# Plain down products for the first token group, down operands made by the second, and four weight sums in three instructions

## The chip, the cores and the metric

The kernel runs on one core of a Trainium2 chip. The metric is the device time of one launch in microseconds, as the median of several runs. The core has TensorE (PE, with its weight loads listed as PEld), VectorE (DVE), ScalarE (ACT) and GpSimd (POOL). SyncE (SP) issues most DMA transfers.

## The reference

The reference is one layer of a hybrid decoder: a mixer with three kinds of heads, then a dense SwiGLU feed-forward part. It works on 2048 prompt tokens with 16 meta tokens ahead of them, and on a sample group of 8 x 4 tokens, with a model width of 1024 and a feed-forward width of 2816. The change is in the feed-forward part alone:

```python
def _swiglu(hn, w_ffn_in, w_ffn_out):
    g, u = jnp.split(hn @ w_ffn_in, 2, axis=-1)
    return (jax.nn.silu(g) * u) @ w_ffn_out
# in _trunk, after the mixer:
h = h + _swiglu(_rmsnorm(h, norm_ffn[l]), w_ffn_in[l], w_ffn_out[l])
```

Inputs and outputs are float32.

## The kernel before

**Precision.** Each operand of a large product is kept as two float16 parts, a high part and the remainder, made by `split_w` (L154): ACT writes the high part (L155) and DVE the remainder (L156). A product is three passes, `PASSES`: high with high, high with low, low with high.

**Fewer products.** The feed-forward products use a 2 x 2 block scheme (Strassen in Winograd's form) with seven block products in place of eight. Seven operands belong to each side: three plain blocks (A11, A12, A22 or B11, B21, B22) and four sums (S1 to S4 or T1 to T4). `left` (L1013) forms the four sums of a gate/up weight tile and `right` (L1021) those of a down weight tile or of the activations, each with four POOL instructions of 128 x 256 elements. `operands` then splits the plain blocks, the last block and the sums.

**Groups.** The 17 token tiles are worked in three groups: tiles 1 to 6, tiles 7 to 12, and tile 0 (48 rows) with tiles 13 to 16. Tiles stand in pairs, so that half a group is 384, 384 and 280 columns. For each group the feed-forward width is cut into four parts of 2, 3, 3 and 3 blocks (`PARTS`), each block being 256 wide. A part has two phases:

- For each block, `hidden` calls `quad` twice, for gate and up. A `quad` runs seven products of 12 matmuls each (L1239) into PSUM banks, with activations as the moving operand, and combines them on ACT, DVE and POOL (L1244 to L1252; L1248 and L1249 are POOL's). `hidden` then applies silu (L1259), multiplies (L1262), forms S1 to S4 of the result on POOL (L1274 to L1280) and splits all seven operands into `hh` (L1268 on ACT, L1269 on DVE).
- For each half m of the output width and each pair of tiles, `down` (L1285) runs seven products (L1292) with `hh` as the stationary and the down weights as the moving operand, 256 columns each. It combines the results into the residual tile `xr` with ACT copies (L1302, L1305), DVE (L1303, L1304, L1324 to L1328) and POOL (L1326, L1329, L1330).

This text calls the place where a part goes from the first phase to the second a turn.

**Weights.** `gu_operands` gives two `w` tiles of 7 KB per partition for each quad, `dn_operands` one tile for each block and half. Both go through `kept`: in the first group the tile is made from the raw weights, used, and written to a DRAM scratch (`wgu_scratch`, `wdn_scratch`). In the later groups it is read back. The raw tiles, the sums and the `w` tiles come from one pool at the left of SBUF. It has 6 raw, 2 sums and 6 `w` buffers in the first group. A new pool with 11 `w` buffers alone is opened ahead of the second group and serves the third too. All these loads and stores are issued by SP, in order.

**Order.** The instructions of each engine stand in a fixed order that a planner writes with its own cost model, from the program order and from the time at which it thinks that operands and buffers are ready. At run time each engine takes its queue in that order.

The activations' operands `x2` are read for the next group while the last part of a group runs (`load_x2`). The residual tiles `xr` are read from a scratch and stored by POOL's queue at the end of a group. In the first two parts of the first group `prep_late` prepares the activations of the last two pairs.

Of the kernel before, what the change touches and what calls it, by code (L numbers as in the profile page):

```python
# [8 lines left out]

F32 = mybir.dt.float32  # L10
F16 = mybir.dt.float16
BF16 = mybir.dt.bfloat16
I32 = mybir.dt.int32
AF = mybir.ActivationFunctionType
# [45 lines left out]
def trunk(ctx, tc, I, O, groups):  # L60
# [4 lines left out]
    def nm(s):  # L65
        n_names[0] += 1
        return f"{s}_{n_names[0]}"
# [933 lines left out]

    A11, A12, A22, S1, S2, S3, S4 = range(7)
    B11, B21, B22, T1, T2, T3, T4 = range(7)

# [3 lines left out]
            split_w(src, hi, lo, scale)  # L1010
        return w

    def left(w, s, a11, a12, a21, a22, plain, scale):  # L1013
        s1, s2, s3, s4 = (s[:, i].rearrange("p (k c) -> p k c", c=a11.shape[-1]) for i in range(4))
        G.tensor_tensor(s1, a21, a22, op=ALU.add)
        G.tensor_tensor(s2, s1, a11, op=ALU.subtract)
        G.tensor_tensor(s3, a11, a21, op=ALU.subtract)
        G.tensor_tensor(s4, a12, s2, op=ALU.subtract)
        return operands(w, plain, a22, s, scale)

    def right(w, s, b11, b12, b21, b22, plain, scale):  # L1021
        G.tensor_tensor(s[:, 0], b12, b11, op=ALU.subtract)
        G.tensor_tensor(s[:, 1], b22, s[:, 0], op=ALU.subtract)
        G.tensor_tensor(s[:, 2], b22, b12, op=ALU.subtract)
        G.tensor_tensor(s[:, 3], b21, s[:, 1], op=ALU.subtract)
        return operands(w, plain, b22.unsqueeze(1), s, scale)

    def pairs(grp):
        big = [t for t in grp if t]
# [80 lines left out]

    pg_cm = tc.tile_pool(name="pg", bufs=1, side="left", reuse_waits="tile")
    pg = [pg_cm.__enter__()]
    w_bufs = [6]

    def raw_tile():
        return pg[0].tile([P, 4, 256], F32, tag="raw", bufs=6, name=nm("raw"))

    def w_full():
        return pg[0].tile([P, 2, 7, 256], F16, tag="w", bufs=w_bufs[0], name=nm("w"))

    def w_tile():
        w = w_full()
# [2 lines left out]
    def sum_tile():  # L1125
        return pg[0].tile([P, 4, 256], F32, tag="sums", bufs=2, name=nm("sums"))

    def kept(dram, make):

        w = w_full()  # L1130
        parts = [w[:, 0], w[:, 1]]
        if w_bufs[0] == 6:
            make(parts)
            nc.sync.dma_start(dram, w.rearrange("p a o c -> p (a o c)"))
        else:
            nc.sync.dma_start(w.rearrange("p a o c -> p (a o c)"), dram)
        return parts
# [4 lines left out]
    def prep_few(x, pst):  # L1142

        L = T0
        n = L // 2
        z2 = [w_full().rearrange("p a o c -> p (a o c)")[:, : 28 * n] for _ in range(2)]

        def put(op, v):
            v = v.rearrange("p (q k) n -> p q k n", q=2)
            hi, lo = (z.rearrange("p (q o k n) -> p q o k n", q=2, o=7, k=2)[:, :, op] for z in z2)  # L1150
            S.activation(hi, v, AF.Copy)
            V.tensor_tensor(lo, v, hi, op=ALU.subtract)

        b12, t1, t2, t3 = (tmp()[:, : 4 * n].rearrange("p (j n) -> p j n", n=n) for _ in range(4))
        for q in range(2):
            ps = pst().rearrange("p (j n) -> p j n", n=P)
            for j in range(4):
                T.transpose(ps[:, j, :L], x[:L, (4 * q + j) * P : (4 * q + j + 1) * P], ident[:L, :L])
            pv = ps[:, :, :n], ps[:, :, n:L]
            if q == 0:  # L1160
                S.activation(b12, pv[1], AF.Copy)
                put(B11, pv[0])
                V.tensor_tensor(t1, b12, pv[0], op=ALU.subtract)
                put(T1, t1)
            else:
                put(B21, pv[0])
                put(B22, pv[1])
                V.tensor_tensor(t2, pv[1], t1, op=ALU.subtract)
                put(T2, t2)
                V.tensor_tensor(t3, pv[1], b12, op=ALU.subtract)  # L1170
# [8 lines left out]
    def gu_operands(c0):  # L1179

        rows = w_gu[:, c0 : c0 + 256].rearrange("(h q k p) c -> q h p k c", h=2, q=2, p=P)

        def make(w, q):
            raw = raw_tile()
            for h in range(2):
                nc.sync.dma_start(raw[:, 2 * h : 2 * h + 2], rows[q, h])
            a = [[raw[:, 2 * h : 2 * h + 2, u * P : (u + 1) * P] for h in range(2)] for u in range(2)]
            left(w, sum_tile(), a[0][0], a[0][1], a[1][0], a[1][1], raw[:, :, 0:P], WG)

        return [kept(wgu_d[c0 % DFF // 256, c0 // DFF, q], lambda w: make(w, q)) for q in range(2)]  # L1190

    def dn_operands(jq, m):


        def make(w):
# [3 lines left out]
            right(w, sum_tile(), raw[:, 0], raw[:, 1], raw[:, 2], raw[:, 3], raw.rearrange("p (k h) c -> p h k c", k=2)[:, 0], WS)  # L1199

        return kept(wdn_d[jq, m], make)

    gu_first = [gu_operands(c) for c in (0, DFF)]
    interleave(outs)
# [4 lines left out]
    with (  # L1209
# [20 lines left out]
        def quad(A, n):  # L1230
# [15 lines left out]
            V.tensor_tensor(r21, prod(S3, T3), r12, op=ALU.add)  # L1246
            S.activation(r22, prod(S1, T1), AF.Copy)  # L1247
            G.tensor_tensor(r12, r12, r22, op=ALU.add)  # L1248
            G.tensor_tensor(r22, r22, r21, op=ALU.add)  # L1249
            V.tensor_tensor(r11, prod(A12, B21), r11, op=ALU.add)  # L1250
# [4 lines left out]
        def hidden(q, jq, n):  # L1255
# [15 lines left out]
            put(A11, a11)  # L1271
            put(A12, a12)
            put(A22, a22)
            G.tensor_tensor(s1, a21, a22, op=ALU.add)  # L1274
            put(S1, s1)
            G.tensor_tensor(s2, s1, a11, op=ALU.subtract)
# [4 lines left out]
            put(S4, s4)  # L1281

        PRODS = ((A11, B11), (S2, T2), (S3, T3), (S1, T1), (A12, B21), (A22, T4), (S4, B22))

        def down(ws, x1, x2_, c, off, L):  # L1285

# [57 lines left out]
        put_off = [pr for pr in all_pairs[early:] if pr[0]] + [[0]]  # L1344

        for gi, grp in enumerate(groups):
            if gi == 1:
                pg_cm.__exit__(None, None, None)
                pg_cm = tc.tile_pool(name="ph", bufs=1, side="left", reuse_waits="tile")
                pg[0] = pg_cm.__enter__()  # L1350
                w_bufs[0] = 11
            n = half[gi]

            rows2 = [[(pr[0], 0, P), (pr[1], 0, P)] if len(pr) == 2 else [(0, 0, T0 // 2), (0, T0 // 2, T0 // 2)] for pr in pairs(grp)]
# [6 lines left out]
            for q0, q1 in PARTS:  # L1361
# [345 lines left out]
```

## Time and profile before

| what | value |
|---|---|
| median of 3 runs | 2410.7 us (2409.39 to 2413.79) |
| the profiled execution | 2401.93 us, span of its instructions 2399.9 us |
| PE busy | 2215.4 us, 92% |
| DVE busy | 1673.4 us, 70% |
| POOL busy | 1148.9 us, 48% |
| ACT busy | 941.8 us, 39% |
| granted TensorE clock, mean | 0.973 |
| moved by DMA | 364.95 MB, 152 GB/s |

In the profile a line number is a line of the kernel, `out<-in` are the program's names without buffer numbers, and an arrow behind an idle time names what ended it. Busy matmuls overlap, so the mean length of one is more than the distance from one to the next. The feed-forward part starts at 1034.6 us of the span. The groups change at 1589.4 and 2043.4 us.

### The profile page before, as it was taken

How to read it: one execution, taken by the hardware profiler on the slowest of the kernel's cores; microseconds unless marked ns; L12 is line 12 of the kernel's file. 1: busy time of each engine (PE TensorE's matmuls, PEld its weight loads, DVE VectorE, ACT ScalarE, POOL GpSimd, SP SyncE). 2: the span in 40 equal slices, each digit the busy share in tenths (PEclk: the TensorE clock that was granted, in tenths of full speed). 3: DMA queues.
4: the chain of work that ended last, by engine and by line, in shares of the span. 5: the costliest groups of instructions: out<-in, count | busy, mean ns of one | idle time of the engine just before them, and what ended most of it. 6: DMA issues, size and time to landing. Idle time of an engine off the chain costs nothing. (4 is left out here: it accounts for less than half of the span.)

```text
span 2399.9 us, 51972 instructions
## 1 busy us (share of the span) xinstructions
PE 2215.4 (92%) x20298; PEld 1605.7 (67%) x20298; DVE 1673.4 (70%) x4064; ACT 941.8 (39%) x2526; POOL 1148.9 (48%) x1595
## 2 busy tenths in 40 slices
PE   6999999999999899787989979789999999999996
PEld 6677767767777445444657566567686867888886
DVE  8789888988988776558778687655454535655546
ACT  7455545545445432334343434422212122332323
POOL 7333233333333364559768787634332324544435
PEclk9999999999999999898999989999999999999998
DMA  7233333333323755995536545684334247744441
GB/s 259 46 67 70 67 74 62 75 65 80 66 65 83 188 192 181 304 305 193 188 140 216 190 169 203 178 305 174 123 121 157 108 168 194 272 176 172 181 166 39
DMA packets 294328, 364.95 MB, mean 152 GB/s; under 512 B 203807, under 2 KB 234479, under 8 KB 294066
## 3 DMA queue, kind: packets, MB, share of 16 engines
q1 hardware_dynamic: 285090, 331.02, 44.2%
q0 software_dynamic: 4384, 15.93, 1.7%
q10 hardware_dynamic: 4608, 14.68, 1.6%
q8 instruction: 159, 2.61, 0.4%
q14 instruction: 87, 0.71, 0.1%
HBM read 212.24 MB, written 103.50 MB: 132 GB/s over the span
## 5 line engine op out<-in xcount | busy, mean ns | idle before, releaser
L1239 PE MATMUL s<-x,w 128*128 128x384 f16 (+1 forms) x5544 | 827.8, 312 | 20.4 <-DMA w<-wgu_scratch 7.8
L1239 PEld LDWEIGHTS <-w 128*128 128x128 f16 x5544 | 543.2, 98 | 302.8 <-issue 19.0
L1292 PE MATMUL dn<-w,hh 128*128 128x256 f16 (+1 forms) x4158 | 446.6, 279 | 54.8 <-ACT hh L1268 21.8
L1292 PEld LDWEIGHTS <-hh 128*128 128x128 f16 (+1 forms) x4158 | 380.6, 99 | 119.6 <-issue 29.5
L212 PEld LDWEIGHTS <-xT 128*128 128x128 f16 (+1 forms) x1992 | 176.1, 99 | 188.6 <-issue 18.2
L1268 ACT ACTIVATE hh<-tmp 128x384 f16<-128x384 f32 (+1 forms) x231 | 112.4, 494 | 282.7 <-DVE tmp L1262 167.4
L1248 POOL TENSOR_TENSOR tmp<-tmp,tmp 128x384 f32<-128x384 f32 (+1 forms) x66 | 67.1, 1017 | 276.3 <-ACT tmp L1247 272.8
L1269 DVE TENSOR_TENSOR hh<-tmp,hh 128x384 f16<-128x384 f32 (+1 forms) x231 | 143.4, 628 | 75.7 <-ACT hh L1268 74.0
L212 PE MATMUL wo<-wo,xT 128*128 128x512 f16 x768 | 176.3, 387 | 7.6 <-DVE xn L992 3.0
L156 DVE SCALAR_TENSOR_TENSOR w<-raw,w 128x512 f16<-128x512 f32 (+1 forms) x136 | 108.5, 830 | 14.2 <-ACT w L155 14.2
L553 POOL TENSOR_TENSOR t<-t 128x8 f32<-128x8 f32 (+2 forms) x100 | 24.9, 249 | 188.2 <-DVE k L551 100.6
L1250 DVE TENSOR_TENSOR tmp<-s,tmp 128x384 f32<-128x384 f32 (+1 forms) x66 | 34.2, 519 | 108.4 <-PE s L1239 108.4
L212 PE MATMUL d<-xT,qf 128*128 128x128 f16 (+1 forms) x1632 | 107.4, 220 | 0.0
L156 DVE SCALAR_TENSOR_TENSOR w<-sums,w 128x1024 f16<-128x1024 f32 x68 | 98.5, 1450 | 9.5 <-ACT w L155 9.4
L1259 ACT ACTIVATE tmp<-tmp 128x384 f32<-128x384 f32 (+1 forms) x132 | 61.6, 490 | 109.0 <-DVE tmp L1250 51.7
L1324 DVE SCALAR_TENSOR_TENSOR xr<-dn,xr 128x256 f32<-128x256 f32 x192 | 78.9, 417 | 35.0 <-PE dn L1292 30.8
L212 PE MATMUL d<-xT,bqk 128*128 128x128 f16 (+1 forms) x1632 | 100.1, 220 | 3.3 <-DVE e L278 3.3
L212 PEld LDWEIGHTS <-qf 128*128 128x128 f16 x1632 | 95.2, 100 | 7.2 <-issue 2.1
L212 PEld LDWEIGHTS <-bqk 128*128 128x128 f16 x1632 | 93.0, 99 | 5.5 <-issue 4.6
L212 PE MATMUL d<-aig,xT 128*128 128x512 f16 (+1 forms) x408 | 92.7, 379 | 3.4 <-DVE g L358 3.4
L212 PE MATMUL d<-bvo,xT 128*128 128x512 f16 (+1 forms) x408 | 95.6, 380 | 0.2 <-DVE qlo L325 0.2
L212 PE MATMUL d<-xT,cq 128*128 128x128 f16 (+1 forms) x1632 | 94.8, 217 | 0.0
(536 smaller groups left out, 4044.2 us busy)
## 6 DMA issues: line engine op xcount, KB each, us to landing
w<-wgu_scratch SPq DMA_DIRECT2D x88, 896.0 KB
wgu_scratch<-w SPq DMA_DIRECT2D x44, 896.0 KB
w<-wdn_scratch SPq DMA_DIRECT2D x44, 896.0 KB
raw<-in_w_ffn_in_dram SPq DMA_DIRECT2D x88, 256.0 KB
wdn_scratch<-w SPq DMA_DIRECT2D x22, 896.0 KB
xs<-in_x_prompt_dram SPq DMA_DIRECT2D x26, 512.0 KB
x_scratch<-pT ACTq DMA_DIRECT2D x28, 448.0 KB
raw<-in_w_ffn_out_dram SPq DMA_DIRECT2D x22, 512.0 KB
```

The source lines that it names most:

```text
L156: V.scalar_tensor_tensor(lo, src, scale, hi, op0=ALU.mult, op1=ALU.subtract)
L212: T.matmul(out, lh(k, a), rh(k, b), start=(n == 0), stop=(n == 3 * nk - 1))
L553: G.tensor_tensor(tn, tv[:, :, :, 0], tv[:, :, :, 1], op=ALU.mult)
L1239: T.matmul(out, A[k // 2][p][:, a, k % 2 * P : k % 2 * P + P], x2[r][:, k // 2, op, k % 2, :n], start=i == 0, stop=i == 11)
L1248: G.tensor_tensor(r12, r12, r22, op=ALU.add)
L1250: V.tensor_tensor(r11, prod(A12, B21), r11, op=ALU.add)
L1259: S.activation(d, d, AF.Silu, scale=UF)
L1268: S.activation(hi, v, AF.Copy)
L1269: V.tensor_tensor(lo, v, hi, op=ALU.subtract)
L1292: T.matmul(out, hh[p][:, q, a, off : off + L], ws[q][r][:, b], start=(q, p, r) == order[0], stop=(q, p, r) == order[-1])
L1324: V.scalar_tensor_tensor(x[:L, cc], m, UD, x[:L, cc], op0=ALU.mult, op1=ALU.add)
```

## The change

- In the first group the down product is plain. `down_plain` computes both tiles of a pair with 512 output columns at a time: for each of the two tiles, each block, each half k of a block and each pass one matmul of 512 columns. One DVE instruction per tile and half adds the result to `xr`. For this the weights are only split (4 of 7 places of a `w` tile), and `hidden` returns after splitting A11, A12, A22 and A21 (in the place of S1).
- The second group makes the seven down operands from the raw weights, as the first did before, and writes them to the scratch. The third group reads them.
- The pools follow: the first stage is as it was, the second has 8 `w`, 3 raw and 2 sums buffers, and a third pool with 11 `w` buffers is opened ahead of the third group.
- The sums of a gate/up weight tile are made by three POOL instructions: one of 128 x 512 elements writes two of them, with a hand-written access pattern, and two of 128 x 256 follow. Two of the sums have the other sign, so `right`, `prep_few` and the pairs in `quad` change signs and places. The sums of a down weight tile are made by three in the same way (`right_of`).

```diff
-    def left(w, s, a11, a12, a21, a22, plain, scale):
-        s1, s2, s3, s4 = (...)
-        G.tensor_tensor(s1, a21, a22, op=ALU.add)
-        G.tensor_tensor(s2, s1, a11, op=ALU.subtract)
-        G.tensor_tensor(s3, a11, a21, op=ALU.subtract)
+    def left(w, s, raw, scale):
+        s3, s2, s4 = (s[:, i].rearrange("p (k c) -> p k c", c=P) for i in (0, 1, 3))
+        a11, a12, a21, a22 = (raw[:, 2 * h : 2 * h + 2, u * P : (u + 1) * P] for u in range(2) for h in range(2))
+        both = AP(a11.tensor, a11.offset, [a11.ap[0], (2 * 256 + P, 2), (256, 2), (1, P)])
+        G.tensor_tensor(s[:, 0::2].rearrange("p i (k c) -> p i k c", c=P), bc(a21, 1, 2), both, op=ALU.subtract)
+        G.tensor_tensor(s2, a22, s3, op=ALU.subtract)
         G.tensor_tensor(s4, a12, s2, op=ALU.subtract)
...
+    def right_of(w, s, b, plain, scale):
+        G.tensor_tensor(s[:, 0::2], b[:, 1::2], b[:, 0:2], op=ALU.subtract)
+        G.tensor_tensor(s[:, 1], b[:, 0], s[:, 2], op=ALU.add)
+        G.tensor_tensor(s[:, 3], b[:, 2], s[:, 1], op=ALU.subtract)
+        return operands(w, plain, b[:, 3].unsqueeze(1), s, scale)
...
-    w_bufs = [6]
+    stage, raw_bufs, w_bufs = [0], [6, 3], [6, 8, 11]
...
     def dn_operands(jq, m):
...
+        if stage[0] == 0:
+            w = w_tile()
+            split_w(load().rearrange("p a c -> p (a c)"), *(z[:, 0:4].rearrange("p a c -> p (a c)") for z in w), WS)
+            return w
+        return kept(wdn_d[jq, m], make, 1)
...
-            V.tensor_tensor(r21, prod(S3, T3), r12, op=ALU.add)
-            S.activation(r22, prod(S1, T1), AF.Copy)
+            V.tensor_tensor(r21, prod(S1, T3), r12, op=ALU.add)
+            S.activation(r22, prod(S3, T1), AF.Copy)
...
             put(A22, a22)
+            if stage[0] == 0:
+                put(A21, a21)
+                return
...
+        def down_plain(ws, x1, x2_, c, off):
+            order = [(q, k, p, r) for q in range(len(ws)) for k in range(2) for p, r in PASSES]
+            for x, ops in ((x1, (A11, A12)), (x2_, (A21, A22))):
+                out = pbt("dn")
+                for o in order:
+                    q, k, p, r = o
+                    T.matmul(out, hh[p][:, q, ops[k], off : off + P], ws[q][r][:, 2 * k : 2 * k + 2].rearrange("p h c -> p (h c)"), start=o == order[0], stop=o == order[-1])
+                V.scalar_tensor_tensor(x[:, c : c + 512], out, UD, x[:, c : c + 512], op0=ALU.mult, op1=ALU.add)
...
-            if gi == 1:
+            if gi:
                 pg_cm.__exit__(None, None, None)
-                pg_cm = tc.tile_pool(name="ph", bufs=1, side="left", reuse_waits="tile")
+                pg_cm = tc.tile_pool(name=f"ph{gi}", bufs=1, side="left", reuse_waits="tile")
                 pg[0] = pg_cm.__enter__()
-                w_bufs[0] = 11
+                stage[0] = gi
...
-                        down(ws, xr[ra], xr[rb], c.start, offs[ra[0]][1], ra[2])
+                        if gi == 0:
+                            down_plain(ws, xr[ra], xr[rb], c.start, offs[ra[0]][1])
+                        else:
+                            down(ws, xr[ra], xr[rb], c.start, offs[ra[0]][1], ra[2])
```

More of the change, by code (lines that the diff above doesn't have):

```diff
@@ L8 @@
 from concourse._compat import with_exitstack
+from concourse.ap import AP
 F32 = mybir.dt.float32
@@ L1011, in operands @@
         return w
-    def left(w, s, a11, a12, a21, a22, plain, scale):
-        s1, s2, s3, s4 = (s[:, i].rearrange("p (k c) -> p k c", c=a11.shape[-1]) for i in range(4))
-        G.tensor_tensor(s1, a21, a22, op=ALU.add)
-        G.tensor_tensor(s2, s1, a11, op=ALU.subtract)
-        G.tensor_tensor(s3, a11, a21, op=ALU.subtract)
+    def left(w, s, raw, scale):
[4 more added lines that the diff above has]
+        G.tensor_tensor(s2, a22, s3, op=ALU.subtract)
         G.tensor_tensor(s4, a12, s2, op=ALU.subtract)
-        return operands(w, plain, a22, s, scale)
+        return operands(w, raw[:, :, 0:P], a22, s, scale)
     def right(w, s, b11, b12, b21, b22, plain, scale):
         G.tensor_tensor(s[:, 0], b12, b11, op=ALU.subtract)
-        G.tensor_tensor(s[:, 1], b22, s[:, 0], op=ALU.subtract)
-        G.tensor_tensor(s[:, 2], b22, b12, op=ALU.subtract)
+        G.tensor_tensor(s[:, 1], b22, s[:, 0], op=ALU.add)
+        G.tensor_tensor(s[:, 2], b22, b12, op=ALU.add)
         G.tensor_tensor(s[:, 3], b21, s[:, 1], op=ALU.subtract)
         return operands(w, plain, b22.unsqueeze(1), s, scale)
+    def right_of(w, s, b, plain, scale):
[3 more added lines that the diff above has]
+        return operands(w, plain, b[:, 3].unsqueeze(1), s, scale)
     def pairs(grp):
@@ L1112, in trunk @@
     pg = [pg_cm.__enter__()]
-    w_bufs = [6]
+    stage, raw_bufs, w_bufs = [0], [6, 3], [6, 8, 11]
     def raw_tile():
-        return pg[0].tile([P, 4, 256], F32, tag="raw", bufs=6, name=nm("raw"))
+        return pg[0].tile([P, 4, 256], F32, tag="raw", bufs=raw_bufs[stage[0]], name=nm("raw"))
     def w_full():
-        return pg[0].tile([P, 2, 7, 256], F16, tag="w", bufs=w_bufs[0], name=nm("w"))
+        return pg[0].tile([P, 2, 7, 256], F16, tag="w", bufs=w_bufs[stage[0]], name=nm("w"))
     def w_tile():
@@ L1126, in sum_tile, with kept @@
         return pg[0].tile([P, 4, 256], F32, tag="sums", bufs=2, name=nm("sums"))
-    def kept(dram, make):
+    def kept(dram, make, when):
         w = w_full()
         parts = [w[:, 0], w[:, 1]]
-        if w_bufs[0] == 6:
+        if stage[0] == when:
             make(parts)
@@ L1167, in prep_few @@
                 put(B22, pv[1])
-                V.tensor_tensor(t2, pv[1], t1, op=ALU.subtract)
+                V.tensor_tensor(t2, pv[1], t1, op=ALU.add)
                 put(T2, t2)
-                V.tensor_tensor(t3, pv[1], b12, op=ALU.subtract)
+                V.tensor_tensor(t3, pv[1], b12, op=ALU.add)
                 put(T3, t3)
@@ L1186, in make, with load @@
                 nc.sync.dma_start(raw[:, 2 * h : 2 * h + 2], rows[q, h])
-            a = [[raw[:, 2 * h : 2 * h + 2, u * P : (u + 1) * P] for h in range(2)] for u in range(2)]
-            left(w, sum_tile(), a[0][0], a[0][1], a[1][0], a[1][1], raw[:, :, 0:P], WG)
-        return [kept(wgu_d[c0 % DFF // 256, c0 // DFF, q], lambda w: make(w, q)) for q in range(2)]
+            left(w, sum_tile(), raw, WG)
+        return [kept(wgu_d[c0 % DFF // 256, c0 // DFF, q], lambda w: make(w, q), 0) for q in range(2)]
     def dn_operands(jq, m):
-        def make(w):
+        def load():
             raw = raw_tile()
@@ L1198, in make @@
             nc.sync.dma_start(raw.rearrange("p (k h) c -> p k (h c)", k=2), w_dn[2 * jq * P : 2 * jq * P + 2 * P, c].rearrange("(k p) c -> p k c", p=P))
-            right(w, sum_tile(), raw[:, 0], raw[:, 1], raw[:, 2], raw[:, 3], raw.rearrange("p (k h) c -> p h k c", k=2)[:, 0], WS)
-        return kept(wdn_d[jq, m], make)
+            return raw
+        def make(w):
+            raw = load()
+            right_of(w, sum_tile(), raw, raw.rearrange("p (k h) c -> p h k c", k=2)[:, 0], WS)
+        if stage[0] == 0:
[3 more added lines that the diff above has]
+        return kept(wdn_d[jq, m], make, 1)
     gu_first = [gu_operands(c) for c in (0, DFF)]
@@ L1283, in trunk @@
         PRODS = ((A11, B11), (S2, T2), (S3, T3), (S1, T1), (A12, B21), (A22, T4), (S4, B22))
+        A21 = S1
+        def down_plain(ws, x1, x2_, c, off):
[6 more added lines that the diff above has]
+                V.scalar_tensor_tensor(x[:, c : c + 512], out, UD, x[:, c : c + 512], op0=ALU.mult, op1=ALU.add)
         def down(ws, x1, x2_, c, off, L):
```

## Prediction, made before the changed kernel was run

> **What bounds the kernel now.** I read the busy times by stage first, to find where TensorE (PE) is not the limit, then the groups of instructions inside those stages, then the order of single instructions at one place where PE stops. The first view is busy time by stretch: PE, PEld, DVE, ACT, POOL, then granted clock, DMA share, GB/s. The rows are the feed-forward part of the first, second and third group of tokens.
>
> ```profile
> 1034.60:1589.40 554.80, 480.57 (x3243) 324.29 (x3241) 415.97 (x640) 223.88 (x444) 429.43 (x447) 0.93 0.58 197
> 1589.40:2043.40 454.00, 453.65 (x3235) 316.83 (x3236) 219.21 (x427) 107.45 (x233) 152.53 (x175) 1.00 0.47 167
> 2043.40:2399.90 356.50, 337.71 (x3236) 283.18 (x3233) 199.13 (x431) 110.38 (x281) 155.37 (x207) 0.98 0.45 169
> ```
>
> The first two groups give PE the same products, yet the first takes 100.8 us longer. The second is PE alone: 453.65 of 454.00 us busy at clock 1.00. The groups of instructions, first group ahead of second, say which products pay (busy, mean ns, then idle before and its releasers):
>
> ```profile
> L1239 PE MATMUL s<-x,w 128*128 128x384 f16 x1848 | 304.3, 327 | 12.6 <-DMA x<-x_scratch 7.3 <-DVE tmp L1252 2.8 <-DVE tmp L1246 2.1
> L1292 PE MATMUL dn<-w,hh 128*128 128x256 f16 x1386 | 176.6, 291 | 53.9 <-ACT hh L1268 21.8 <-DVE hh L1269 8.8 <-DVE xr L1324 6.9
> ...
> L1239 PE MATMUL s<-x,w 128*128 128x384 f16 x1848 | 302.6, 327 | 7.8 <-DMA w<-wgu_scratch 7.8
> L1292 PE MATMUL dn<-w,hh 128*128 128x256 f16 x1386 | 152.3, 273 | 0.3 <-DVE hh L1269 0.3
> ```
>
> The gate/up products (L1239) differ by 1.7 us busy and 5.3 us of idle beyond a start wait of 7.3 us. The down products (L1292) differ by 24.3 us busy (slow clock, waits inside groups) and 53.6 us idle. Another 7.8 us is the wait that ends the first group and that the view books to the second. So the time is lost where a part turns from gate/up to down. One such turn, from the instructions in order of time:
>
> ```profile
> 1383.45 0.82 PE L1292 MATMUL dn<-w,hh 128*128 128x256 f16 x6
> 1390.54 1.04 PE L1292 MATMUL dn<-w,hh 128*128 128x256 f16 x4 [5.75 <-ACT hh L1268]
> 1395.13 7.68 PE L1292 MATMUL dn<-w,hh 128*128 128x256 f16 x55 [3.55 <-DVE hh L1269]
> 1404.85 5.12 PE L1292 MATMUL dn<-w,hh 128*128 128x256 f16 x30 [2.04 <-ACT hh L1268]
> ...
> 1386.44 1.70 POOL L1023 TENSOR_TENSOR sums<-raw,sums 128x256 f32<-128x256 f32 x1
> 1391.27 0.72 POOL L1025 TENSOR_TENSOR sums<-raw,sums 128x256 f32<-128x256 f32 x1
> 1391.95 0.99 POOL L1248 TENSOR_TENSOR tmp<-tmp,tmp 128x384 f32<-128x384 f32 x1
> ...
> 1385.83 1.74 DVE L156 SCALAR_TENSOR_TENSOR w<-sums,w 128x1024 f16<-128x1024 f32 x1
> 1394.04 0.56 DVE L1262 SCALAR_TENSOR_TENSOR tmp<-tmp,tmp 128x384 f32<-128x384 f32 x1 [4.12 <-POOL tmp L1249]
> ```
>
> PE waits for hh. hh waits for the last gate/up combination (POOL L1248, then DVE L1262), and that stands in POOL's queue behind the sums of down weights (L1022 to L1025), in DVE's behind their splits (L156). The second group has the same hh chain and no operand making, and PE passes the same turn without a stop:
>
> ```profile
> 1755.77 41.43 PE L1292 MATMUL dn<-w,hh 128*128 128x256 f16 x378
> ```
>
> **The change, part by part.** Prices for the first group (means under that load):
>
> ```profile
> L156 DVE SCALAR_TENSOR_TENSOR w<-sums,w 128x1024 f16<-128x1024 f32 x64 | 92.6, 1448 | 6.1 <-ACT w L155 6.0
> L156 DVE SCALAR_TENSOR_TENSOR w<-raw,w 128x512 f16<-128x512 f32 x64 | 58.1, 907 | 13.7 <-ACT w L155 13.6
> L156 DVE SCALAR_TENSOR_TENSOR w<-raw,w 128x256 f16<-128x256 f32 x64 | 47.2, 737 | 0.0
> L1023 POOL TENSOR_TENSOR sums<-raw,sums 128x256 f32<-128x256 f32 x24 | 25.9, 1080 | 0.0
> L1276 POOL TENSOR_TENSOR tmp<-tmp,tmp 128x384 f32<-128x384 f32 x11 | 14.9, 1359 | 0.0
> L1330 POOL TENSOR_TENSOR xr<-xr,tmp 128x256 f32<-128x256 f32 x24 | 20.5, 855 | 1.0
> ...
> 1314.32 0.99 POOL L1249 TENSOR_TENSOR tmp<-tmp,tmp 128x384 f32<-128x384 f32 x1
> 1315.27 0.73 POOL L1016 TENSOR_TENSOR sums<-sums,raw 128x256 f32<-128x256 f32 x1
> ...
> 963.01 27.80 PE L212 MATMUL wo<-wo,xT 128*128 128x512 f16 x128
> L998 DVE SCALAR_TENSOR_TENSOR xs<-wo,xs 128x512 f32<-128x512 f32 x20 | 13.5, 684 | 8.3 <-DMA xs<-in_x_prompt_dram 5.1 <-PE wo L212 3.1
> ```
>
> *Plain down, PE (on the path).* Per down tile and pass, 7 matmuls of 256 columns become 4 of 512: 1386 become 792. A 512-column matmul takes 27.80/128 = 0.217 us in the output projection, so 792 x 0.217 = 172 us against 152.3 undisturbed and 176.6 + 53.9 now: the bare price is +20 us. In a sentence by itself: the Trainium skill, TensorE: Matmul & The Clock Gate, section Back-to-back issue gap, gives a sustained 131 ns at 512 columns, by which the down products would be 104 us by estimate; the same section's isolated 216 ns is what this trace shows, so the trace decides.
>
> *What leaves the first group's engines (beside PE).* Sums of the 22 down tiles, 4 POOL instructions each: 88 x about 1.0 = 90 us. The hidden sums, 4 x 11 x about 1.3 = 57 us of POOL, and 3 of 7 hh splits. Seven-part recombination per pair and half (24 times): 3 POOL adds of 0.86 us (62 us), 2 ACT copies, and on DVE 8 instructions become 2 of 0.68 us. Splits of a down tile on DVE go from 0.91 + 0.74 + 1.45 = 3.1 us to one of 1.45. POOL, 429 us busy, falls by about 210. The chain at the turn loses both things that it queued behind: no POOL sums of down weights, and no S1 to S4. The plain products take A11 and A12 first, 18 matmuls (3.9 us) for one tile before A21 is wanted, which is the cover for the last combination.
>
> *Three instructions for four sums.* Two 128x256 become one of 512 elements. From 0.73 at 256 and 0.99 at 384 the line gives 1.25 us against 1.46: 0.2 us x 44 = 9 us of POOL. No row has this access pattern: bounds are 0.99 and 2 x 0.73 each, at most 11 us of POOL either way over 22 more; nothing of it is on the path, since POOL then has half its time free. If that cover is gone it is 0.2 us per tile.
>
> *First group, sum.* PE 302.6 + 172, start wait 7.3, wait at the end 7.8: 490 us. Of the remaining stalls (5.3 + 53.6 idle, 24 us slow) I keep 10 us, 2 to 3 per turn, for what is left of the chain: 500 against 554.8, **-55 us**. Bounds: 0 kept is -65, half kept is -26.
>
> *Second group: down operands are made here.* Added on 22 tiles: raw load of 512 KB, 3 POOL sums, 3 ACT and 3 DVE splits, a store of 896 KB in place of a load:
>
> ```profile
> w<-wdn_scratch SPq DMA_DIRECT2D x44, 896.0 KB
> raw<-in_w_ffn_out_dram SPq DMA_DIRECT2D x22, 512.0 KB
> ```
>
> By first-group prices DVE +22 x 3.1 = 68 us (219 to 287 of 454), POOL +22 x 3.0 = 66 (153 to 219). Both stay under two thirds, where the first group ran at 75 and 77%. With 8 w buffers a down tile's slot falls free when the gate/up tile eight before it is done, so the last two of six can be made 14 us (one quad of 82/6 us) ahead of the turn. Bounds for PE: 0 (they finish in that time), or a third of the first group's down-turn loss (77.9 us at 66 tiles made, here 22): 26. It is nearer the light end, since the slots open earlier: **+10 us**.
>
> *SP's queue.* The stores wait for DVE, and gate/up loads stand behind them. Those are due two quads (27 us) later, so I cost this at nothing; uncovered it is one load, 8 us, a time. Bytes rise by 22 x 512 KB, 11.5 MB, beside 167 GB/s x 454 us = 76 MB now, and the first group moved 197 GB/s: nothing.
>
> *Third buffer stage.* A new pool opens before the third group. The same happens now before the second:
>
> ```profile
> 1581.31 5.58 SPq L1136 DMA_DIRECT2D w<-wgu_scratch x8
> 1589.44 56.41 PE L1239 MATMUL s<-x,w 128*128 128x384 f16 x336 [7.84 <-DMA w<-wgu_scratch]
> ...
> 2021.24 4.24 SPq L1136 DMA_DIRECT2D w<-wgu_scratch x5
> 2043.36 1.83 PE L1239 MATMUL s<-x,w 128*128 128x280 f16 x14
> ```
>
> There the first load goes out when the last down product ends and PE waits 7.84 us; before the third group loads run 22 us ahead and nothing waits. 66 tiles over 8 slots end on slot 1, so slot 0 of the new pool lies under a down weight used to the last. **+8 us**, bounds 0 and 14 (if x2 loads collide).
>
> *Sum.* -55 + 10 + 8 = -37 us. The profiled execution is 2401.9 us (span 2399.9), 8.8 under the median 2410.7; taken off the median: **2374 us**.
>
> **The rivals.**
> *A, the making moves its stalls along (slower).* At the second group's turns the down sums and splits again stand ahead of L1248 and L1262. For it: the order of each queue is fixed ahead, and the 5.75 us stop above is just such an order. Against: a third of the tiles, and earlier slots. If each of the four turns loses what it lost in the first group: -55 + 78 + 8 = +31, 2442 us. It decides from 47 us in the second group, 12 per turn. The Trainium skill, SBUF — State Buffer, section SBUF: two separate sides, says that POOL and a two-input DVE instruction exclude each other for a whole instruction; L1016 at 0.73 alone and L1023 at 1.70 beside DVE's splits agree, and it speaks for this rival.
> *B, half of the first group's turn loss stays.* hh still needs the whole last combination, down splits still stand in DVE's queue: -26 + 10 + 8 = -8, 2403 us. Also the clock: the 55 matmuls after the stops took 7.68 us, 140 ns each against 41.43/378 = 110. In a sentence by itself: the Trainium skill, TensorE: Matmul & The Clock Gate, section What's actually happening, has the clock halve after an idle window of 3.4 us, so that only stops shorter than that are cheap; the trace agrees in direction.
> *C, everything is hidden.* No stall at any turn, prefetch before the third group kept: -65 - 0 = 2346 us.
> *D, the products are no fewer limits.* If the first group were bound by PE already, plain products would cost +20 and nothing return: 2411 + 38. The 53.9 us idle speak against it.
>
> **How the numbers follow.** Forecast 0.62 (own range 2352 to 2396), C 0.12, B 0.12, A 0.12, D 0.02. Range 2344 to 2404 leaves out A, D and the upper part of B. A change of 0.2% (5 us) is about what a measurement here can tell. Faster: forecast, C and half of B, 0.80; the same: a third of B, 0.04; slower: A, D and the rest, 0.16.
>
> **What would show it.** Right: the first group's feed-forward stretch is near 500 us with POOL under half busy, 792 down matmuls of 512 columns near 0.217 us each, idle before them under 15 us; the second group near 464 with down sums on POOL well ahead of L1248; a DMA wait near 8 us at the third group's first gate/up product. Wrong: idle before the down products of the second group above 47 us (A), or of the first above 30 us (B). An unlooked-for wait at SP, a gate/up load held behind a store of down operands, would break the forecast too.

## The result, and the profile after

The changed kernel takes 2364.8 us (median of 4 runs, 2361.7 to 2369.5) against 2410.1 us for the kernel before in the same series. The ratio is 0.983, 95% interval [0.9808, 0.9854], which is 35 to 46 us less. The profiled execution of the changed kernel took 2369.5 us (span 2367.8), the longest of its runs. That of the kernel before took 2401.9 us, less than any of its other four runs (2406.1 to 2413.8), so the two traces are only 32.1 us apart.

Busy time by stretch of the changed kernel, for the feed-forward part of the first, second and third group (PE, PEld, DVE, ACT, POOL, then granted clock, DMA share, GB/s):

```profile
1051.20:1531.30 480.10, 472.55 (x2649) 258.62 (x2647) 294.03 (x421) 174.68 (x319) 206.70 (x204) 1.00 0.55 184
1531.30:2008.40 477.10, 460.01 (x3234) 317.47 (x3234) 279.32 (x497) 143.86 (x302) 235.23 (x244) 0.99 0.48 168
2008.40:2367.80 359.40, 340.56 (x3234) 284.52 (x3234) 195.42 (x423) 110.05 (x279) 152.35 (x202) 0.97 0.48 184
```

In the kernel before, the row of the first group (shown in the prediction) held 9.7 us (1034.6 to 1044.3) in which PE had begun and then waited for activations. From 1044.3 its groups lasted 545.1, 453.9 and 356.5 us. Against these the first group is 65.0 us shorter, the second 23.2 longer and the third 2.9 longer. The feed-forward part begins 6.9 us later. Together that is the -32.1 us.

The groups of instructions (busy, mean ns, then idle before and its releasers), first group ahead of second. L1319 is the plain down product, L1329 the seven-product one, L1021 and L1036 the new first sums of a gate/up and of a down weight tile:

```profile
L1319 PE MATMUL dn<-w,hh 128*128 128x512 f16 x792 | 171.9, 379 | 2.2 <-ACT w L156 1.3 <-ACT hh L1290 0.6 <-DVE hh L1291 0.3
L1021 POOL TENSOR_TENSOR sums<-raw 128x512 f32<-128x512 f32 x40 | 68.8, 1721 | 136.8 <-DVE w L157 115.0 <-DMA raw<-in_w_ffn_in_dram 21.7
...
L1329 PE MATMUL dn<-w,hh 128*128 128x256 f16 x1386 | 157.7, 276 | 12.3 <-DVE hh L1291 11.5 <-ACT hh L1290 0.5
L1036 POOL TENSOR_TENSOR sums<-raw 128x512 f32<-128x512 f32 x22 | 40.7, 1849 | 53.3 <-DVE w L157 43.8 <-DMA raw<-in_w_ffn_out_dram 9.5
```

In the first group the idle time before the down products fell from 53.9 to 2.2 us. In the second it rose from 0.3 to 12.3, and the products themselves took 5.4 us more. PE in order of time shows two turns, one of the first group and one of the second, and both changes of group. L1261 is the gate/up product. The last row of such a view counts matmuls only as far as the view reaches, here and below:

```profile
1479.18 46.78 PE L1319 MATMUL dn<-w,hh 128*128 128x512 f16 x216
1531.31 57.22 PE L1261 MATMUL s<-x,w 128*128 128x384 f16 x336 [5.35 <-DMA w<-wgu_scratch]
...
1704.86 1.57 PE L1329 MATMUL dn<-w,hh 128*128 128x256 f16 x11
1709.74 41.92 PE L1329 MATMUL dn<-w,hh 128*128 128x256 f16 x367 [3.31 <-DVE hh L1291]
...
2008.42 43.02 PE L1261 MATMUL s<-x,w 128*128 128x280 f16 x336 [4.84 <-DMA w<-wgu_scratch]
```

The turn at 1704.9 passed without a stop before (378 matmuls in 41.43 us). Now it stops after 11 matmuls. POOL and DVE at that place, in order of time:

```profile
1701.24 1.74 DVE L157 SCALAR_TENSOR_TENSOR w<-sums,w 128x1024 f16<-128x1024 f32 x1
1701.98 1.59 POOL L1038 TENSOR_TENSOR sums<-raw,sums 128x256 f32<-128x256 f32 x1
...
1703.53 1.27 POOL L1036 TENSOR_TENSOR sums<-raw 128x512 f32<-128x512 f32 x1
...
1704.87 0.92 POOL L1037 TENSOR_TENSOR sums<-raw,sums 128x256 f32<-128x256 f32 x1
...
1705.87 0.72 POOL L1038 TENSOR_TENSOR sums<-raw,sums 128x256 f32<-128x256 f32 x1
1706.56 0.99 POOL L1270 TENSOR_TENSOR tmp<-tmp,tmp 128x384 f32<-128x384 f32 x1
1707.63 0.99 POOL L1271 TENSOR_TENSOR tmp<-tmp,tmp 128x384 f32<-128x384 f32 x1
1708.65 0.56 DVE L1284 SCALAR_TENSOR_TENSOR tmp<-tmp,tmp 128x384 f32<-128x384 f32 x1 [3.44 <-POOL tmp L1271]
```

This is the stop that the first group had before, one group later. The three sums of a down tile (L1036 to L1038) stand in POOL's queue ahead of the last gate/up combination (L1270, L1271). DVE's L1284 waits 3.44 us for that, the operands `hh` wait for DVE, and PE waits for `hh`.

### The profile page after: what moved, and what is told of

It is laid out like the page before. It is cut to its first block, busy times and chain, and to the rows that moved or that the text cites. A ratio compares the mean times of both kernels' runs of the same rounds, so it can differ in the third digit from the quotient of the medians.

```text
span 2367.8 us, 50283 instructions
## 1 busy us (share of the span) xinstructions
PE 2234.6 (94%) x19704; PEld 1551.4 (66%) x19704; DVE 1609.8 (68%) x3909; ACT 928.4 (39%) x2467; POOL 1006.8 (43%) x1413
## 5 line engine op out<-in xcount | busy, mean ns | idle before, releaser
L1261 PE MATMUL s<-x,w 128*128 128x384 f16 (+1 forms) x5544 | 828.1, 313 | 10.2 <-DMA w<-wgu_scratch 10.2
L1261 PEld LDWEIGHTS <-w 128*128 128x128 f16 x5544 | 544.2, 98 | 292.9 <-DMA w<-wgu_scratch 11.0
L1329 PE MATMUL dn<-w,hh 128*128 128x256 f16 (+1 forms) x2772 | 275.4, 274 | 12.9 <-DVE hh L1291 11.5
L1329 PEld LDWEIGHTS <-hh 128*128 128x128 f16 (+1 forms) x2772 | 238.6, 98 | 48.9 <-DVE hh L1291 14.3
L213 PE MATMUL wo<-wo,xT 128*128 128x512 f16 x768 | 184.8, 401 | 12.6 <-DVE xs L999 6.5
L1290 ACT ACTIVATE hh<-tmp 128x384 f16<-128x384 f32 (+1 forms) x198 | 95.6, 489 | 229.9 <-DVE tmp L1284 155.1
L1270 POOL TENSOR_TENSOR tmp<-tmp,tmp 128x384 f32<-128x384 f32 (+1 forms) x66 | 63.4, 961 | 268.6 <-ACT tmp L1269 238.0
L1319 PE MATMUL dn<-w,hh 128*128 128x512 f16 x792 | 171.9, 379 | 2.2 <-ACT w L156 1.3
L1291 DVE TENSOR_TENSOR hh<-tmp,hh 128x384 f16<-128x384 f32 (+1 forms) x198 | 119.3, 609 | 49.7 <-ACT hh L1290 48.4
L157 DVE SCALAR_TENSOR_TENSOR w<-raw,w 128x512 f16<-128x512 f32 (+2 forms) x158 | 129.6, 846 | 28.0 <-ACT w L156 28.0
L1319 PEld LDWEIGHTS <-hh 128*128 128x128 f16 x792 | 77.3, 98 | 95.7 <-issue 1.3
L1021 POOL TENSOR_TENSOR sums<-raw 128x512 f32<-128x512 f32 x44 | 74.9, 1702 | 150.4 <-DVE w L157 117.1
L156 ACT ACTIVATE w<-raw 128x512 f16<-128x512 f32 (+2 forms) x158 | 84.7, 583 | 98.8 <-PE dn L1319 62.4
```

The costliest lines, as they stand in the source:

```text
L156: S.activation(hi, src, AF.Copy, scale=scale)
L157: V.scalar_tensor_tensor(lo, src, scale, hi, op0=ALU.mult, op1=ALU.subtract)
L213: T.matmul(out, lh(k, a), rh(k, b), start=(n == 0), stop=(n == 3 * nk - 1))
L1021: G.tensor_tensor(s[:, 0::2].rearrange("p i (k c) -> p i k c", c=P), bc(a21, 1, 2), both, op=ALU.subtract)
L1261: T.matmul(out, A[k // 2][p][:, a, k % 2 * P : k % 2 * P + P], x2[r][:, k // 2, op, k % 2, :n], start=i == 0, stop=i == 11)
L1319: T.matmul(out, hh[p][:, q, ops[k], off : off + P], ws[q][r][:, 2 * k : 2 * k + 2].rearrange("p h c -> p (h c)"), start=o == order[0], sto ...
```

## The experiments

The diffs are against the changed kernel, or from the run with both pools kept on against the version just before, and show only the main lines.

**The new sums alone (third part of the change).** The kernel before with the three-instruction sums and turned signs; seven-product down and making stay in the first group, and there is no third pool.

```diff
-    stage, raw_bufs, w_bufs = [0], [6, 3], [6, 8, 11]
+    stage, raw_bufs, w_bufs = [0], [6], [6, 11]
...
-        return kept(wdn_d[jq, m], make, 1)
+        return kept(wdn_d[jq, m], make, 0)
```

> The third part alone: seven products in every group and down operands made by the first group, as before, but all weight sums in three instructions with the turned signs. Theory (the gain is the plain product and what it takes off POOL and DVE at the first group's turns): the three instructions save about 0.4 us of POOL per weight tile, some of it ahead of the last combination at the turns, so -2 to -6 us against before, ratio 0.998 to 1.000. Rival (POOL's queue is all of the turn loss, so fewer and shorter instructions there give much of the gain): -15 us or more, ratio 0.994 or less.

Measured: 2408.2 us, ratio 1.0023 [1.0008, 1.0039]. Busy time by stretch of this kernel, first group:

```profile
1053.46:1602.78 549.32, 482.79 (x3244) 326.10 (x3242) 423.78 (x639) 223.28 (x444) 402.48 (x384) 0.93 0.57 197
```

Its groups of instructions there, the down product and the new first sum of a gate/up tile:

```profile
L1326 PE MATMUL dn<-w,hh 128*128 128x256 f16 x1386 | 181.4, 296 | 54.7 <-ACT hh L1290 22.3 <-DVE hh L1291 8.4 <-DVE tmp L1337 5.0
...
L1021 POOL TENSOR_TENSOR sums<-raw 128x512 f32<-128x512 f32 x40 | 69.1, 1728 | 54.4 <-DVE w L157 50.5 <-DMA raw<-in_w_ffn_in_dram 3.8
```

POOL is 27 us less busy (429 to 402), but the idle time before the down products stays at 54.7 us (53.9 before). From the point where PE no longer waits for activations the group lasts 546.3 us against 545.1. So a little less work on POOL was worth nothing here, where the sums still stand ahead of the last combination. Both theories expected a gain and both fell. In the two profiles the loss lies ahead of the first group (1056.5 us for 1044.3), a start that varies, as the last run shows.

**Seven products everywhere, made by both groups.** The changed kernel with the plain products taken out: the first group makes the seven down operands for itself, the second makes them again and stores them.

```diff
-            split_w(load().rearrange("p a c -> p (a c)"), ...)
+            make(w)
...
-                        if gi == 0:
+                        if False:
                             down_plain(...)
```

> The second part without the first: both the first and the second group make the seven down operands, only the second stores them, pools as in the changed kernel, seven products everywhere. Theory: the first group stays as in the kernel with the three-instruction sums alone, the second pays 18 us at its turns and 5 us at the new pool, so +20 to +25 us against that kernel, near 2430 us, ratio 1.006 to 1.010. Rival (the second group's 23 us came from elsewhere, as from the new timing of loads behind a shorter first group): within 5 us of the three-instruction kernel.

Measured: 2436.9 us, ratio 1.0133 [1.0114, 1.0152]. Busy time by stretch, first and second group:

```profile
1054.30:1600.30 546.00, 480.67 (x3244) 324.83 (x3242) 425.66 (x640) 222.96 (x444) 403.10 (x385) 0.93 0.47 161
1600.30:2075.58 475.28, 458.42 (x3234) 316.51 (x3234) 285.40 (x499) 144.19 (x301) 234.88 (x245) 0.99 0.48 171
```

The second group costs 21.0 us more than with the sums alone (454.3), a wait of 4.72 us for gate/up weights at the third group's start included, and the third group 1.6 us more. That is the price of making there. By the medians this run is 29 us above the sums alone, more than the 20 to 25 expected; no trace shows where the rest lies. Against the changed kernel the second and third group differ by under 2 us and the first by 65.9 (546.0 against 480.1). That is what plain products without making are worth. No run divides it between the sums of down weights, S1 to S4 and the recombination. The first group lasts as long as with the sums alone (546.3), though it stores no down operands here, so those stores cost nothing there.

**Four instructions for the sums.** The changed kernel with the first, two-output sum as two instructions again:

```diff
-        G.tensor_tensor(s[:, 0::2], b[:, 1::2], b[:, 0:2], op=ALU.subtract)
+        G.tensor_tensor(s[:, 0], b[:, 1], b[:, 0], op=ALU.subtract)
+        G.tensor_tensor(s[:, 2], b[:, 3], b[:, 1], op=ALU.subtract)
```

> The changed kernel with the weight sums by four instructions of 128x256 again, the signs left turned. Theory: the first group is bound by PE and has POOL to spare, so nothing there; at the second group's turns two makings stand ahead of the last combination, each longer by about 0.4 us, so +0 to +4 us against the changed kernel, ratio to before 0.981 to 0.985. Rival (three instructions carry a good part of the gain): +10 us or more, ratio 0.987 or more.

Measured: 2368.1 us, ratio 0.9852 [0.983, 0.9874], 3.3 us above the changed kernel by the medians, with intervals that overlap. Its first and second group take 2.2 and 2.8 us more (482.3 and 479.9). The third part is worth 0 to 5 us beside the others and was not seen alone.

**Plain products in both groups, making in the third.** The down operands are made in the third group and never stored.

```diff
-                        if gi == 0:
+                        if gi <= 1:
                             down_plain(...)
```

> Plain products in the first and the second group, down operands made by the third and never stored, 8 w and 3 raw buffers in the second and third stages. Theory: in the second group plain products cost +20 us of PE and take away 18 us of turn loss; the third group then has the making on it, 22 tiles in 357 us instead of 477, and loses 18 to 30 us at its turns: +15 to +30 us against the changed kernel, ratio 0.988 to 0.995. Rival (the second group's loss isn't its making, so it stays): +38 to +50 us.

Measured: 2405.3 us, ratio 0.9998 [0.9985, 1.0011]: 40 us more than the changed kernel. PE in order of time, the starts of the second and third group:

```profile
1530.37 57.62 PE L1263 MATMUL s<-x,w 128*128 128x384 f16 x336 [6.16 <-DMA w<-wgu_scratch]
...
2013.62 16.58 PE L1263 MATMUL s<-x,w 128*128 128x280 f16 x122 [8.98 <-DMA w<-wgu_scratch]
```

From the groups of instructions of the third group, the down products:

```profile
L1331 PE MATMUL dn<-w,hh 128*128 128x256 f16 x924 | 115.3, 289 | 20.0 <-ACT hh L1292 15.9 <-DVE tmp L1275 2.3 <-DVE hh L1293 1.6
```

The second group takes 483.3 us, 6.1 more than with making: the bare +20 us of plain products and a longer wait at its end, less the stops at its turns. The third group takes 391.6 us against 359.4. Its parts are shorter (280 columns for 384), so the same making is a larger share of each, and PE stops for 20.0 us before its down products. The 40 us are over what I expected and in the rival's range, but not by the rival's cause: the second group has no stop at its turns, and most of the loss stands in the third, where the making went.

**The second group's down sums left out.** The sums are not formed, and the raw values are split in their place, so the kernel's outputs are other numbers; loads, splits and stores stay.

```diff
         def make(w):
             raw = load()
+            operands(w, raw.rearrange("p (k h) c -> p h k c", k=2)[:, 0], raw[:, 3].unsqueeze(1), raw, WS)
+            return
             right_of(...)
```

> The changed kernel with the second group's POOL sums of down weights left out: the raw tile is split in their place, so the down products of the second and third groups are of other numbers. The splits, loads, stores and buffers stay. Theory (at the second group's turns POOL's makings stand ahead of the last combination, and that is the 18 us): the second group's down idle falls from 12 to under 3 us and the time by 12 to 18 us against the changed kernel, ratio to before 0.975 to 0.979. Rival (DVE's splits ahead of L1284 and L1291 hold it): idle stays above 8 us, time within 5 us of the changed kernel.

Measured: 2353.9 us, ratio 0.9781 [0.9752, 0.9811]. PE in order of time, one turn of the second group and the start of the third:

```profile
1707.04 41.43 PE L1331 MATMUL dn<-w,hh 128*128 128x256 f16 x378
...
1999.62 30.56 PE L1263 MATMUL s<-x,w 128*128 128x280 f16 x243 [4.82 <-DMA w<-wgu_scratch]
```

The turn is whole again, and the second group takes 460.0 us, 17.1 less, with the same wait at its end. So POOL's sums stop PE at the second group's turns, not the splits, the stores or SP. This run takes away both their place in the queue and their work; the runs below keep the work and change the place.

**No new pool ahead of the third group.** The second pool, 8 `w` buffers, serves the third group too.

```diff
-            if gi:
+            stage[0] = gi
+            if gi == 1:
```

> The changed kernel without a new pool ahead of the third group: the second stage's pool with 8 w buffers is kept. Theory (the first load of the third group waits for the slot of a down weight used to the last): the 4.8 us wait at the start of the third group goes, and 8 buffers are deep enough: -3 to -6 us against the changed kernel, 0.9805 to 0.982. Rival (the depth of 11 is needed, or the queue order of SP sets it): no gain or a loss.

Measured: 2358.5 us, ratio 0.9806 [0.9785, 0.9827]. PE in order of time, the starts of the second and the third group:

```profile
1527.62 56.53 PE L1261 MATMUL s<-x,w 128*128 128x384 f16 x336 [6.21 <-DMA w<-wgu_scratch]
...
1998.36 40.20 PE L1261 MATMUL s<-x,w 128*128 128x280 f16 x336
```

The wait at the third group's start is gone and the third group takes 356.5 us (2354.9 - 1998.4), as in the kernel before. So the new pool costs 4.8 us of wait and 2.9 us in the group itself: 7.7 us. The 2.9 us are slower matmuls behind the stop. The first 336 of the group took 43.02 us in the changed kernel and 40.20 here, and busy time by stretch shows the first 6.6 us of the group, changed kernel ahead of this run:

```profile
2008.40:2015.00 6.60, 6.58 (x32) 4.41 (x33) 2.83 (x4) 0.70 (x2) 3.72 (x8) 0.56 1.02 422
...
1998.40:2005.00 6.60, 6.60 (x58) 5.41 (x56) 4.90 (x10) 2.02 (x6) 4.42 (x10) 1.00 0.91 303
```

The same time held 32 matmuls at a granted clock of 0.56 behind the stop, and 58 at 1.00 without it.

**Down operands in buffers of their own.** In the second group 4 buffers for gate/up and 6 for down operands, 2 raw and 1 sums.

```diff
+        if stage[0] == 1:
+            return pg[0].tile([P, 2, 7, 256], F16, tag="wd" if own else "w", bufs=6 if own else 4, name=nm("w"))
```

> The changed kernel with buffers of their own for the down operands in the second group: 4 for gate/up, 6 for down, 2 raw, 1 sums, in place of 8 shared w, 3 raw, 2 sums. The making can start a part earlier, and the planner's POOL order then has no making between the last two quads and the turn, from the second part on. Theory (queue order at the turn): 12 to 18 us less than the changed kernel, ratio 0.975 to 0.979; gate/up loads two quads ahead still suffice. Rival (4 gate/up buffers are too few, PE waits for DMA): slower than the changed kernel.

Measured: 2354.4 us, ratio 0.9787 [0.9765, 0.9809]. PE in order of time at the first turn of the second group:

```profile
1587.25 0.93 PE L1331 MATMUL dn<-w,hh 128*128 128x256 f16 x7
1591.37 0.61 PE L1331 MATMUL dn<-w,hh 128*128 128x256 f16 x4 [3.19 <-ACT hh L1292]
...
1625.95 82.06 PE L1263 MATMUL s<-x,w 128*128 128x384 f16 x504
```

The second group takes 466.6 us. Turns two to four pass without a stop (378 matmuls in 41.43 us each), though POOL still makes all sums. The first turn lasts 38.7 us where 28.2 would do.

**The same buffers, both pools kept through the third group.** The six down buffers lie in a pool of their own, and no pool is opened ahead of the third group.

```diff
+            stage[0] = gi
+            if gi == 1:
...
+                pd_cm = tc.tile_pool(name="phd", bufs=1, side="left", reuse_waits="tile")
+                pg.append(pd_cm.__enter__())
```

> The same buffers as in the kernel with 4 and 6, but the six down buffers in a pool of their own that lies lowest, and both pools kept through the third group, so that gate/up slots at both changes of group lie under memory free early. Theory: the turns' 12 to 18 us and both DMA waits (5.3 and 4.8 us) go: 2338 to 2350 us where the changed kernel has 2365, ratio 0.970 to 0.976. Rival (the waits at the changes of group are set by SP's order and x2, not by the slots): no better than the kernel with 4 and 6 alone.

Measured: 2349.7 us, ratio 0.9773 [0.975, 0.9796]. In order of time, PE at the second group's start, POOL near the first turn, and SP's queue ahead of the group:

```profile
1531.02 57.28 PE L1263 MATMUL s<-x,w 128*128 128x384 f16 x336 [5.41 <-DMA w<-wgu_scratch]
...
1591.19 1.58 POOL L1036 TENSOR_TENSOR sums<-raw 128x512 f32<-128x512 f32 x1
1592.72 1.31 POOL L1273 TENSOR_TENSOR tmp<-tmp,tmp 128x384 f32<-128x384 f32 x1
...
1513.72 8.53 SPq L1408 DMA_DIRECT2D xr<-h_scratch  x3
1522.35 1.94 SPq L1153 DMA_DIRECT2D w<-wgu_scratch  x4
```

POOL's rows show why the first turn still stops: the last combination (L1273) at 1592.7 stands behind sums of later down tiles. SP's rows show why PE still waits at the group's start. The loads of the residual rows `xr` (L1408) wait for the stores of the group before, and the first gate/up load of the new group stands behind them, at 1522.4. The wait at the third group's start is gone, that at the second's is not: I expected both to go, and on the second group's the rival was right. The second group takes 465.3 us. In the changed kernel the same place in SP's queue, and what its load waited for behind the residual loads, read:

```profile
1514.08 8.55 SPq L1404 DMA_DIRECT2D xr<-h_scratch  x3
1524.75 4.57 SPq L1151 DMA_DIRECT2D w<-wgu_scratch  x8
...
SPq L1151 <- PE dn L1319: 2.1, 1, 2.1
```

There the load waited another 2.1 us for one of the first group's last down products, which is the wait for the slot that the prediction spoke of. So two things hold back this load, and freeing the slot alone leaves the residual loads.

**Parts of 3, 3, 3 and 2 blocks in the second group.**

```diff
-            for q0, q1 in PARTS:
+            for q0, q1 in ([(0, 3), (3, 6), (6, 9), (9, 11)] if gi == 1 else PARTS):
```

> The version with own down buffers kept through the third group, and in the second group the parts are 3, 3, 3 and 2 blocks instead of 2, 3, 3 and 3; all else is as in that version. There the first turn of the second group still lost about 10 us (38.7 us from the first down product of the turn to its end where 28.2 would do), since all six down slots are free at once and only two blocks of gate/up products stand ahead of the turn, so that sums of the next part's down weights lie between its last combinations. Theory: with three blocks ahead of the first turn these sums are done sooner, the first turn passes without a stop, and the second group falls by 8 to 10 us, from 465.3 to about 456 (a DMA wait of 5.4 at its start kept): 2340 us, 0.973. Rival: the shorter last part gives the loads of the third group's tokens (about 20 us of SP's queue) less time, and what is won at the first turn is lost as a DMA wait of 5 to 10 us at the start of the third group: 2348 us, no change.

Measured: 2343.2 us, ratio 0.976 [0.9732, 0.9787]. PE in order of time, the second group's first part and the third group's start:

```profile
1527.77 84.81 PE L1263 MATMUL s<-x,w 128*128 128x384 f16 x504 [5.76 <-DMA w<-wgu_scratch]
1612.42 41.43 PE L1331 MATMUL dn<-w,hh 128*128 128x256 f16 x378
...
1982.78 20.90 PE L1263 MATMUL s<-x,w 128*128 128x280 f16 x174
```

The first turn passes whole and the second group takes 455.0 us (465.3 before this step, 453.9 with no making at all). POOL still makes all 22 tiles' sums in this group, so it is where they stand in its queue that stopped PE. The third group starts without a wait and meets one of 1.28 us in its first half, a small part of the rival. By the medians the step is 6.4 us, and the intervals overlap; its worth is read from the group's length.

**The residual loads on ACT's queue.**

```diff
-                    nc.sync.dma_start(*xr_loads.pop())
+                    (nc.scalar if gi else nc.sync).dma_start(*xr_loads.pop())
```

> As the version with the parts of 3, 3, 3 and 2 blocks, and the loads of the residual rows (xr) of the second and third group are issued by ACT's queue instead of SP's, where they stood ahead of the first gate/up load and waited for the store of the group before. Theory: the first gate/up load of the second group goes out some 5 to 9 us sooner and the wait of 5.4 us at the start of the second group goes: 5 us less than the version with SP, about 2335 us, 0.971. Rival: ACT now stands at these loads until the store is done, the first gate/up outputs are not taken off PSUM meanwhile, and PE waits for ACT instead by as much or more: 0 to 10 us slower than the version with SP.

Measured: 2336.3 us, ratio 0.9718 [0.9698, 0.9738]. In order of time, PE at the second group's first part and SP's queue ahead of it:

```profile
1520.50 55.74 PE L1263 MATMUL s<-x,w 128*128 128x384 f16 x342
1577.09 26.54 PE L1263 MATMUL s<-x,w 128*128 128x384 f16 x162 [0.85 <-DMA w<-wgu_scratch]
...
1498.15 2.78 SPq L1153 DMA_DIRECT2D w<-wgu_scratch  x4
```

The first gate/up load goes out 22 us ahead of its use, and the wait of 5.8 us at the start of the second group is gone. ACT does wait for the stores now, up to 6.6 us, but at a place where PE has products to do. This is the fastest version by the medians, 28.5 us below the changed kernel.

**A second profile of the kernel before.**

> The kernel before, unchanged, for a second profile of it. In its first profile the first group's feed-forward products start at 1044.3 us, in the profiles of all changed versions between 1044 and 1058. Theory: this start varies from execution to execution by some 10 us whatever the kernel, the second profile shows it elsewhere than 1044.3 (1047 to 1058), and the three groups then last 545, 454 and 356 us again within 2 us each. Rival: it is a property of the kernel before (its order in the attention part differs), and it starts at 1044 again within 1 us; then 3 to 10 us of each changed version's time is lost ahead of the first group.

Measured, PE in order of time:

```profile
1033.93 0.33 PE L1239 MATMUL s<-x,w 128*128 128x384 f16 x1
1035.18 1.14 PE L1239 MATMUL s<-x,w 128*128 128x384 f16 x6 [0.93 <-DMA x<-x_scratch]
1036.58 53.62 PE L1239 MATMUL s<-x,w 128*128 128x384 f16 x329 [0.26 <-DMA x<-x_scratch]
...
1581.08 56.23 PE L1239 MATMUL s<-x,w 128*128 128x384 f16 x336 [6.54 <-DMA w<-wgu_scratch]
...
2034.82 25.43 PE L1239 MATMUL s<-x,w 128*128 128x280 f16 x212
```

The groups last 544.5, 453.7 and 356.6 us, within 1 us of the first profile, so the stage lengths used here repeat. The start does vary, by 7.8 us between two executions of one kernel. But it moved the other way than I expected: 1036.6, where the changed versions run without a stop from between 1047 and 1058. What sets it is not settled. One place shows that it comes from earlier in the span: the first sum for the activations' operands, in the kernel before and in the changed kernel (POOL in order of time).

```profile
850.70 0.77 POOL L1022 TENSOR_TENSOR pb<-xs,xs 128x256 f32<-128x256 f32 x1
```

```profile
860.96 0.76 POOL L1028 TENSOR_TENSOR pb<-xs,xs 128x256 f32<-128x256 f32 x1
```

Up to there PE, POOL, DVE and ACT hold the same instructions in the same order in both kernels, and the changed one is already 10 us behind. So the 6.9 us by which its feed-forward part begins later in the first pair of traces don't come from the instructions that the change altered. The second profile of the kernel before has this sum at 850.9, the changed versions between 852.2 and 862.1. From this sum to the first uninterrupted product the kernel before took 194 and 186 us, the changed versions 189 to 202. No experiment took this apart.

## Why the prediction was right

The forecast was 2374 us, -37 us; measured were 2365 us and -35 to -46 us. Its mechanism, a gain of the first group's turns paid for in small part by the second group's, is what the traces show. That the sum came so near is in part luck: the first group gained 10 us more than forecast, the second lost 8 us more, and the two errors nearly cancel.

- **Plain products, +20 us bare.** 792 matmuls took 171.9 us, 0.217 us each, against 172 foreseen. The Trainium skill, TensorE: Matmul & The Clock Gate, section Back-to-back issue gap, gives a sustained 131 ns at 512 columns; this trace does not agree, and the section's isolated 216 ns fits.
- **First group, -55 us forecast, -65 measured.** The mis-sized term is the 10 us of stalls that I kept. 2.2 us are left: with POOL at 206.7 of 480.1 us and no down sums or S1 to S4 in its queue, PE passes the turn at 1479.2 whole. A further 2.5 us came from a shorter wait at the group's end (5.35 for 7.84), a wait that was 6.54 in the second profile of the kernel before, so this part is scatter in some measure. The forecast length of 500 us also held a start wait of 7.3 us, which the changed kernel's profile does not have; the -65 us leave the start out on both sides. The granted clock rose from 0.93 to 1.00 with the stops gone. The Trainium skill, TensorE: Matmul & The Clock Gate, section What's actually happening, ties the clock to idle windows; the trace agrees in direction, and no run here separates the clock from the stops.
- **Second group, +10 us forecast, +18.4 measured** (477.1 less the wait of 4.84, against 453.9). The mechanism was in rival A. I placed the making well ahead of the turn since slots fall free early, and that step failed: the sums of two down tiles stood directly ahead of the last combination (POOL at 1701 to 1706), and leaving the sums out returned 17.1 us. It stays far under the 47 us at which A would have decided. L1038 took 1.59 us beside DVE's 1.74 us split and 0.72 us without one. The Trainium skill, SBUF — State Buffer, section SBUF: two separate sides, has a POOL instruction and a DVE instruction with two SBUF inputs exclude each other; the trace agrees in direction.
- **Third pool, +8 us forecast, 7.7 measured**: 4.84 as a wait and 2.9 as slower matmuls behind it, both gone with one pool. The forecast was a wait of 7.84 alone, so the cause was right, and that the sum agrees is chance.
- **Three-instruction sums.** I took 1.25 us for the two-output instruction. It takes 1.27 us in the quickest rows and 1.7 us on average under load. Put in alone, it took 27 us from POOL's busy time in the first group, 0.44 us for each of 62 tiles where I had 0.2. That nothing of it lies on the path held as far as the runs can tell: alone it brought no gain, and without it the changed kernel was 3.3 us slower, not clear of noise.
- **SP's queue, costed at nothing.** For stores of down operands that held: PE's only DMA waits in the changed kernel's second and third group stand at their starts. What I had not named is that the residual loads stand ahead of the first gate/up load of a group. At the second group's start the load waited for them and then 2.1 us more for its slot; the wait of PE went when the slot was free early and the residual loads were moved too. Moving them alone in the changed kernel was not run.

Of the rivals, C (everything hidden, 2346 us) asked that no turn stops. It is no property of the hardware that it failed: with own buffers, other parts and the residual loads moved, the second group does its making in 453.3 us, and 2336 us is below C's time.

## What to carry to other kernels

When work is taken off a busy stage, find first which queue holds up the critical instruction there: the order in the queue, more than the engine's share of busy time, decided the losses at the turns here (POOL was under half busy in the second group and still stopped PE at its turns). Work that is moved to a stage with spare time may need buffers of its own: here six for the down operands let the last three of the four turns pass whole, and a longer first part the first one too. And at a change of stage, look at what stands ahead of the next stage's first load in the DMA-issuing queue: here a load that waited for a store held up the next stage's first weights behind it.

## What the runs showed beyond expectation

The POOL instruction that writes two sums at once stretches from 1.27 us to 1.72 and 1.85 us on average in the groups where DVE splits weights. The start of the feed-forward part differs by up to 22 us between profiled executions of all versions (1036.6 to 1058.3), while the lengths of the groups repeat within 1 us in the two profiles of the kernel before, so versions a few us apart were better compared by stage than by span.
